# An expert's way back to the tokens: its products placed nine pieces after its last one instead of five

## The chip, the cores and the metric

The kernel runs on one core of one Trainium2 chip. The time is that of the device for one execution, in microseconds (us); three runs of the kernel before gave 1337.02, 1337.85 and 1338.05 us.

## What is computed

A trunk of two residual layers over 256 tokens of width 1024, in float32. Layer 0 is attention beside a short convolution and then a dense SwiGLU; layer 1 is a gated recurrence and then a mixture of experts: each token goes to two of eight SwiGLU experts. The change lies in the mixture of experts, of which the reference says

```
def moe_swiglu(h, w_router, w_gate, w_up, w_down):
    ...
    def expert_block(args):
        tok, e = args
        xb = xf[tok]
        hb = jax.nn.silu(xb @ w_gate[e]) * (xb @ w_up[e])
        return hb @ w_down[e]
    yb = lax.map(expert_block, (row_tok.reshape(n_blocks, MOE_BLOCK), blk_expert))
    y = yb.reshape(n_rows, D).astype(jnp.float32) * row_gate[:, None]
    out = jnp.zeros((T, D), jnp.float32).at[row_tok].add(y)
```

The last line is the one that matters here: an expert's rows, scaled by their gates, are added at their tokens.

## The kernel before

**Pieces and blocks.** The experts' stage begins about 500 us into the execution and takes the rest of it. An expert's hidden width of 3584 is cut into seven parts of 512, and a block is one part of one expert, 56 blocks in all. The loop at the end of `experts` walks a list of pieces; a block has twelve: g0 to g3 (gate), u0 to u3 (up) and d0 to d3 (the down products of the block ahead of it). A piece is half of a 1 MB load of weights. Three of the eight experts are heavy (up to 128 rows, three matmuls for each slice of weights: lines L240 to L242) and five light (up to 64 rows, whose high and low halves share one matmul, L1101 and L1102). After a lead of three heavy blocks the order is light, heavy, light, and again light, heavy, light, so two light blocks stand between heavy ones.

**Weights.** Weights are split into a high and a low part so that the fast float32 form of the matmul keeps its precision: ScalarE (ACT) writes the high part H (L260), VectorE (DVE) subtracts it from the weights and writes the low part L (L261). There are four pairs of H and L. `prepare` is called in the loop so that a load is split about four loads (eight pieces) ahead of its matmuls; ACT has to wait until TensorE (PE) has done with the pair that it is to overwrite. SyncE (SP) issues the loads; a tile of weights is free for the next load once DVE has subtracted.

**The order.** Every engine takes its instructions in the order in which the loop writes them. For a piece n the loop writes the matmuls of the piece, then what `follow` hangs on it, then what was put off to this n by `at(n, ...)`, then the `prepare` that is due. So DVE's work for a step that hangs on piece n stands in DVE's queue behind the subtraction of a load that PE will use about three to four loads later.

**Steps that share the two tiles z.** PSUM has two tiles with the tag z (`pz`), taken in turn. They are used by
- the turn of a finished hidden part, five pieces after u3, which is g0 of the next block: for a heavy block `turn`, four transposes (L1129), then a split of the result by ACT and DVE (L260 and L261 on a tile of 512 columns); for a light block `turn_light`, sixteen matmuls with an identity (L1140), then ACT's Silu (L1145) and DVE's product (L1146);
- the gathering of an expert's rows, and `factors` and `back` (L1082, L1091), a block ahead of an expert's start;
- `combine`, the step that the change moves: it takes a quarter of an expert's output, brings its rows back to the tokens with four matmuls of 256 columns (two each of L1170 and L1171) into a tile z, and DVE adds the tile to `x_sb` (L1173), which frees it.

**When an expert ends.** Its last down pieces d0 to d3 lie in the block that follows its last one. After d1 and after d3 `out_parts` scales half of the output (ACT L1162, DVE L1163). The four calls of `combine` are put off from there:

```
                end = n + BACK + 7 >= len(pieces)
                for j in R2:
                    at(n + (1 + j if end else BACK + 2 * j + i - 1), combine, p, i - 1 + j)
```

Counted from d1 with BACK at 5 they hang on the pieces 5, 7, 9 and 11 further on: g2, u0, u2 and d0 of the block after. Experts 1 and 0 end in blocks that follow each other, and so do 4 and 3: there eight calls stand in two light blocks. Experts 2 and 5 end alone, and their calls stand in a heavy block. Experts 7 and 6 are the last, and `end` gives them short distances.

Of the kernel before, what the change touches and what calls it, by code (L numbers as in the profile page):

```python
# [54 lines left out]
FIRST = 1  # L55
SECOND = 2
TURN = 5
BACK = 5

TURNS8 = N_RING + 2  # L60
TURNS4 = TURNS8 + 2
# [54 lines left out]
def body(ctx, tc, x_d, w_d, prm_d, bv_d, rt_d, out_d):  # L116
# [811 lines left out]
    def experts(rest):  # L928
# [249 lines left out]
        def at(n, fn, *a):  # L1178
            later.setdefault(min(n, len(pieces) - 1), []).append((fn, a))

        def follow(n):
# [22 lines left out]
            elif m == "d" and i % 2 and f == NF - 1:  # L1204
                out_parts(p, i // 2)
# [5 lines that stand above are left out]
# [152 lines left out]
```

## Time and profile before

| | |
|---|---|
| median of three runs | 1337.85 us |
| profiled execution: its own time | 1336.78 us |
| profiled execution: span of the trace | 1334.8 us |
| PE, DVE, ACT: busy share of the span | 97%, 85%, 73% |
| adds of `combine` (L1173) | 32, from 686.9 us to 1328.2 us |
| granted clock of TensorE, mean over the span | 0.994 of full speed |

The busy share of PE is not its share of useful work, since matmuls overlap in the trace: a wait is read from the bracket behind an instruction, which gives the idle time ahead of it and the instruction that ended it. Where an engine is busy without a break for tens of us it sets the pace there, or another engine hands it its work just in time.

### The profile page before, as it was taken

The numbers are of one execution on the slowest core, as the hardware profiler recorded it, in microseconds if no ns is written. First come the engines' busy times: TensorE is split into PE (matmuls) and PEld (weight loads), VectorE is DVE, ScalarE is ACT, GpSimd is POOL, SyncE is SP. The second block draws the span as 40 slices with busy tenths as digits, with TensorE's granted clock in tenths as the row PEclk, the third lists the DMA queues.
The fourth block names the chain that finished last, engine by engine and source line by source line (L and its number), as shares of the span: only waits on it lengthen the run. The fifth ranks groups of instructions, "written<-read, shape, count | busy, mean of one in ns | idle before, by whom it ended". The sixth has DMA issues, their size and how long they took to land.

```text
span 1334.8 us, 19883 instructions
## 1 busy us (share of the span) xinstructions
PE 1293.1 (97%) x7727; PEld 1134.4 (85%) x7727; DVE 1135.0 (85%) x1051; ACT 971.6 (73%) x937; POOL 4.2 (0%) x29
## 2 busy tenths in 40 slices
PE   8899999999998999999999999999999999999997
PEld 7799999999998877888877888878887888888885
DVE  6677655555688787999999999999989999999996
ACT  6455433444578687888888898889888898889883
POOL 1000000000000000000000000000000000000000
PEclk9899999999999999999999999999999999999999
DMA  7434545555443778999999999999999999999993
GB/s 302 174 127 158 190 177 176 186 190 189 138 179 107 273 273 325 400 421 422 421 416 381 416 421 420 415 406 422 420 422 393 390 422 421 422 406 423 421 420 121
DMA packets 61446, 427.19 MB, mean 320 GB/s; under 512 B 7200, under 2 KB 7200, under 8 KB 11296
## 3 DMA queue, kind: packets, MB, share of 16 engines
q1 hardware_dynamic: 60624, 425.22, 79.9%
q8 instruction: 62, 1.02, 0.3%
q10 hardware_dynamic: 720, 0.62, 0.1%
q14 instruction: 40, 0.33, 0.1%
HBM read 424.77 MB, written 1.05 MB: 319 GB/s over the span
## 4 chain that ended last, share of the span: by engine, by line
PE 76%; DVE 13%; issue 5%; ACT 4%; DMA 1%; SPq 0%; DVEq 0%; ACTq 0%
PE pw L240 11%; PE pw L241 11%; PE pw L242 10%; DVE L L261 9%; PE pw L1101 5%; PE pw L1102 5%; PE pz L1140 4%; PE pa L1101 3%; PE pa L241 3%; PE pa L1102 3%; PE pa L242 3%; PE pa L240 3%; PE pa L323 3%; PE pa L322 3%; PE pa L321 3%
## 5 line engine op out<-in xcount | busy, mean ns | idle before, releaser
L261 DVE TENSOR_TENSOR L<-w,H 128x2048 fp32r<-128x2048 f32 (+1 forms) x243 | 536.6, 2239 | 27.2 <-ACT H L260 27.0
L260 ACT ACTIVATE H<-w 128x2048 fp32r<-128x2048 f32 (+1 forms) x243 | 451.0, 1878 | 50.3 <-PE pw L242 19.0
L233 ACT ACTIVATE H<-w 128x1024 fp32r<-128x1024 f32 (+1 forms) x138 | 140.8, 1041 | 153.6 <-issue 140.6
L261 DVE TENSOR_TENSOR L<-b,H 128x2048 fp32r<-128x2048 f32 (+1 forms) x102 | 222.3, 2200 | 7.7 <-ACT H L260 7.7
L1101 PE MATMUL pw<-H,b 128*128 128x512 f32 x560 | 222.3, 397 | 0.0
L1102 PE MATMUL pw<-L,b 128*128 128x512 f32 x560 | 219.0, 391 | 0.2
L234 DVE TENSOR_TENSOR L<-w,H 128x1024 fp32r<-128x1024 f32 (+1 forms) x138 | 164.1, 1205 | 62.0 <-ACT H L233 62.0
L260 ACT ACTIVATE H<-b 128x2048 fp32r<-128x2048 f32 (+1 forms) x102 | 186.7, 1845 | 20.4 <-PE pw L242 9.6
L240 PE MATMUL pw<-b,H 128*128 128x256 f32 x672 | 191.7, 286 | 2.3 <-DVE b L600 1.1
L241 PE MATMUL pw<-b,H 128*128 128x256 f32 x672 | 191.4, 285 | 0.0
L242 PE MATMUL pw<-b,L 128*128 128x256 f32 x672 | 191.1, 284 | 0.0
L240 PE MATMUL pw<-H,b 128*128 128x512 f32 x336 | 135.0, 402 | 1.4 <-ACT b L1057 1.1
L241 PE MATMUL pw<-L,b 128*128 128x512 f32 x336 | 133.2, 397 | 1.2 <-DVE L L261 1.2
L240 PEld LDWEIGHTS pw<-b,H 128*128 128x128 f32 x672 | 129.7, 193 | 3.9 <-issue 3.1
L242 PE MATMUL pw<-H,b 128*128 128x512 f32 x336 | 131.8, 392 | 0.1
L241 PEld LDWEIGHTS pw<-b,H 128*128 128x128 f32 x672 | 129.7, 193 | 0.2
L242 PEld LDWEIGHTS pw<-b,L 128*128 128x128 f32 x672 | 129.8, 193 | 0.0
L1102 PEld LDWEIGHTS pw<-L,b 128*128 128x128 f32 x560 | 105.3, 188 | 21.8 <-DVE L L261 1.6
L1101 PEld LDWEIGHTS pw<-H,b 128*128 128x128 f32 x560 | 105.3, 188 | 20.2
L1101 PE MATMUL pa<-H,b 128*128 128x512 f32 x280 | 109.7, 392 | 0.0
L1102 PE MATMUL pa<-L,b 128*128 128x512 f32 x280 | 109.1, 390 | 0.0
L322 PE MATMUL pa<-b,H 128*128 128x256 f32 x352 | 99.4, 284 | 1.5 <-DVE b L261 1.5
(250 smaller groups left out, 1925.3 us busy)
## 6 DMA issues: line engine op xcount, KB each, us to landing
w<-in_w_dram SPq DMA_DIRECT2D x297, 1024.0 KB, 8.9
b<-in_w_dram SPq DMA_DIRECT2D x94, 1024.0 KB, 9.4
w<-in_w_dram SPq DMA_DIRECT2D x12, 512.0 KB, 11.2
b<-in_w_dram SPq DMA_DIRECT2D x8, 512.0 KB, 9.6
w<-in_w_dram SPq DMA_DIRECT2D x4, 768.0 KB, 8.0
x_sb<-in_x_dram SPq DMA_DIRECT2D x4, 256.0 KB, 7.7
out_dram<-x_sb SPq DMA_DIRECT2D x2, 256.0 KB, 3.1
out_dram<-x_sb ACTq DMA_DIRECT2D x2, 256.0 KB, 3.1
```

Of the source, the lines that this page charges most:

```text
L233: A.activation(h, w[:, c], AF.Copy)
L234: V.tensor_sub(l, w[:, c], h.bitcast(F32))
L240: T.matmul(o, a[0], b[0], start=first, stop=False)
L241: T.matmul(o, a[0], b[1], start=False, stop=False)
L242: ended[:] = [T.matmul(o, a[1], b[0], start=False, stop=last)]
L260: A.activation(oh, src, AF.Copy)
L261: V.tensor_sub(ol, src, oh.bitcast(F32))
L321: T.matmul(o, h[:, c], m[0][:, ks[i], :], start=f and d % 2 == 0, stop=False, skip_group_check=True)
L322: T.matmul(o, h[:, c], m[1][:, ks[i], :], start=False, stop=False, skip_group_check=True)
L1101: T.matmul(o, a, h, start=first, stop=False)
L1102: T.matmul(o, a, l, start=False, stop=last)
L1140: T.matmul(o[:, c:c + 64], src[:, k * P:(k + 1) * P], ii, start=True, stop=True)
```

## The change

One number that sets the order of the work:

```diff
--- before.py
+++ after.py
@@ -55,7 +55,7 @@
 FIRST = 1
 SECOND = 2
 TURN = 5
-BACK = 5
+BACK = 9
```

The four calls of `combine` now hang on the pieces 9, 11, 13 and 15 after d1: u2, d0 and d2 of the block after, and g0 of the one after that. The calls of experts 7 and 6 keep their places, since `end` holds for them with either number. So 24 of the 32 calls move, each with its four matmuls on PE and its add on DVE. No instruction is added or taken away, and no load changes its place among the loads.

On DVE, where experts 1 and 0 end: the stretch from behind the subtraction for d0 and d1 of a block to the product that belongs to the turn in g0 of the next block (L1146). `L` are the low parts of loads, `x_sb` is the sum that `combine` adds to. Before:

```order
L1173 TENSOR_TENSOR x_sb<-pz_6802,x_sb 128x512
L261 TENSOR_TENSOR L_6817<-w_6814,H_6816 128x2048
L1173 TENSOR_TENSOR x_sb<-pz_6825,x_sb 128x512
L261 TENSOR_TENSOR L_6838<-w_6835,H_6837 128x2048
L1173 TENSOR_TENSOR x_sb<-pz_6845,x_sb 128x512
L261 TENSOR_TENSOR L_6860<-w_6857,H_6859 128x2048
L1173 TENSOR_TENSOR x_sb<-pz_6869,x_sb 128x512
L1163 SCALAR_TENSOR_TENSOR b_895_6882<-pa_5250,gs_5084,b_894_6881 128x512
L261 TENSOR_TENSOR L_6888<-w_6885,H_6887 128x2048
L1163 SCALAR_TENSOR_TENSOR b_895_6882<-pa_5251,gs_5084,b_894_6881 128x512
L261 TENSOR_TENSOR L_6908<-b_899_6905,H_6907 128x2048
L1146 TENSOR_TENSOR b_904_6925<-pz_6916,b_904_6925 128x256
```

and now, at the same place:

```order
L261 TENSOR_TENSOR L_6811<-w_6808,H_6810 128x2048
L261 TENSOR_TENSOR L_6826<-w_6823,H_6825 128x2048
L1173 TENSOR_TENSOR x_sb<-pz_6833,x_sb 128x512
L261 TENSOR_TENSOR L_6848<-w_6845,H_6847 128x2048
L1173 TENSOR_TENSOR x_sb<-pz_6857,x_sb 128x512
L1163 SCALAR_TENSOR_TENSOR b_893_6870<-pa_5250,gs_5084,b_892_6869 128x512
L261 TENSOR_TENSOR L_6876<-w_6873,H_6875 128x2048
L1173 TENSOR_TENSOR x_sb<-pz_6885,x_sb 128x512
L1163 SCALAR_TENSOR_TENSOR b_893_6870<-pa_5251,gs_5084,b_892_6869 128x512
L261 TENSOR_TENSOR L_6902<-b_898_6899,H_6901 128x2048
L1173 TENSOR_TENSOR x_sb<-pz_6910,x_sb 128x512
L1146 TENSOR_TENSOR b_904_6925<-pz_6916,b_904_6925 128x256
```

The instructions are the same; each of the four adds has moved two subtractions back, and the third and the fourth now stand around the last subtraction ahead of L1146.

On PE, the end of g0 of the block after that, where the turn of a light block stands. `pz` are the tiles z in the order in which they are taken. Before, the turn follows the piece, and the latest `combine` was four pieces earlier:

```order
L1102 MATMUL pw_6911<-L_6838,b_512_5129 128x512
L1140 MATMUL pz_6916<-ii,b_879_6812 128x64 [waits DVE_49]
L1140 MATMUL pz_6916<-ii,b_879_6812 128x64 x3
L1140 MATMUL pz_6916<-ii,b_889_6855 128x64 [waits Activation_49]
L1140 MATMUL pz_6916<-ii,b_889_6855 128x64 x3
```

and now:

```order
L1102 MATMUL pw_6905<-L_6826,b_512_5129 128x512
L1170 MATMUL pz_6910<-b_568_5410,b_863_6748 128x256 [waits DVE_49]
L1171 MATMUL pz_6910<-b_568_5410,b_864_6749 128x256
L1170 MATMUL pz_6910<-b_568_5410,b_863_6748 128x256
L1171 MATMUL pz_6910<-b_568_5410,b_864_6749 128x256
L1140 MATMUL pz_6916<-ii,b_878_6806 128x64 [waits DVE_49]
L1140 MATMUL pz_6916<-ii,b_878_6806 128x64 x3
```

The fourth `combine` (tile 6910) now stands directly ahead of the turn (tile 6916), and the tile z that the turn takes is the one that the third `combine` (tile 6885) has filled two pieces earlier.

Where an expert ends alone, the same happens to a heavy block's turn. PE before:

```order
L1102 MATMUL pw_8266<-L_8202,b_1075_7679 128x512
L1129 MATMUL pz_8271<-ident,b_1181_8169 128x128 [waits DVE_49]
L1129 MATMUL pz_8271<-ident,b_1181_8169 128x128 x3
L1101 MATMUL pw_8266<-H_8201,b_1075_7679 128x512
L1102 MATMUL pw_8266<-L_8202,b_1075_7679 128x512
```

and now:

```order
L1102 MATMUL pw_8260<-L_8190,b_1075_7679 128x512
L1170 MATMUL pz_8265<-b_575_5442,b_1166_8094 128x256 [waits DVE_49]
L1171 MATMUL pz_8265<-b_575_5442,b_1167_8095 128x256
L1170 MATMUL pz_8265<-b_575_5442,b_1166_8094 128x256
L1171 MATMUL pz_8265<-b_575_5442,b_1167_8095 128x256
L1129 MATMUL pz_8271<-ident,b_1180_8163 128x128 [waits DVE_49]
L1129 MATMUL pz_8271<-ident,b_1180_8163 128x128 x3
```

Here too the fourth `combine` (tile 8265) comes between g0's products and the turn (tile 8271).

## Rows read from the trace of the kernel before

**Rows 1.** Chain that ended last, in time: start us, us, engine, tile, line

```profile
661.78 1.73 PE pz L1140 x16
...
712.85 1.73 PE pz L1140 x16
...
755.98 1.73 PE pz L1140 x16
...
847.06 1.73 PE pz L1140 x16
...
893.02 1.73 PE pz L1140 x16
...
982.71 1.73 PE pz L1140 x16
...
1033.78 1.73 PE pz L1140 x16
```

**Rows 2.** Windows: us, busy of PE, PEld, DVE, ACT, POOL; PEclk, DMA, GB/s

```profile
680.00:690.00 10.00, 7.97 (x40) 6.18 (x39) 10.00 (x8) 7.89 (x8) 0.00 (x0) 1.00 1.01 421
...
700.00:710.00 10.00, 9.23 (x46) 6.96 (x45) 10.00 (x8) 8.24 (x8) 0.00 (x0) 1.00 0.98 381
```

**Rows 3.** Timeline of DVE, experts 1 and 0: start us, us, line [idle before]

```profile
684.68 2.28 DVE L261 TENSOR_TENSOR L<-w,H 128x2048 fp32r<-128x2048 f32 x1
686.88 0.68 DVE L1173 TENSOR_TENSOR x_sb<-pz,x_sb 128x512 f32<-128x512 f32 x1
...
695.88 0.74 DVE L1163 SCALAR_TENSOR_TENSOR b<-pa,gs,b 128x512 fp32r<-128x512 f32 x1
...
701.60 0.41 DVE L1146 TENSOR_TENSOR b<-pz,b 128x256 f32<-128x256 f32 x1
701.93 2.28 DVE L261 TENSOR_TENSOR L<-b,H 128x2048 fp32r<-128x2048 f32 x1
...
721.60 2.29 DVE L261 TENSOR_TENSOR L<-b,H 128x2048 fp32r<-128x2048 f32 x1 [0.78 <-ACT H L260]
```

**Rows 4.** Timeline of PE, the same stretch

```profile
684.82 0.39 PE L1170 MATMUL pz<-b,b 128*128 128x256 f32 x1 [1.82 <-DVE b L261]
...
696.01 1.89 PE L1140 MATMUL pz<-ii,b 128*128 128x64 f32 x16
...
712.69 1.89 PE L1140 MATMUL pz<-ii,b 128*128 128x64 f32 x16
```

**Rows 5.** Timeline of ACT: the split behind the first turn

```profile
698.69 1.92 ACT L260 ACTIVATE H<-b 128x2048 fp32r<-128x2048 f32 x1 [0.36 <-PE pw L1101]
```

**Rows 6.** Timeline of DVE, then of PE, where expert 2 ends

```profile
853.76 2.28 DVE L261 TENSOR_TENSOR L<-w,H 128x2048 fp32r<-128x2048 f32 x1
...
864.79 0.60 PE L1129 MATMUL pz<-ident,b 128*128 128x128 f32 x4
865.14 0.47 PE L1101 MATMUL pw<-H,b 128*128 128x512 f32 x1
...
872.15 0.39 PE L240 MATMUL pa<-H,b 128*128 128x512 f32 x1
873.23 0.50 PE L241 MATMUL pa<-L,b 128*128 128x512 f32 x1 [0.69 <-DVE L L261]
```

**Rows 7.** Timeline of PE: other waits, and matmuls behind one

```profile
40.81 0.27 PE L460 MATMUL pa<-dmb,slope 128*128 128x128 bf16 x1 [3.32 <-DVE b L423]
...
503.26 0.66 PE L1091 MATMUL pz<-ident,b 128*128 128x128 f32 x4 [1.94 <-DVE gs L1085]
...
503.99 0.60 PE L241 MATMUL pw<-L,b 128*128 128x512 f32 x1
...
507.37 0.43 PE L241 MATMUL pw<-L,b 128*128 128x512 f32 x1
```

**Rows 8.** Windows as in rows 2, behind two of PE's waits

```profile
40.00:45.00 5.00, 3.59 (x16) 3.00 (x17) 4.82 (x14) 1.01 (x3) 0.00 (x0) 0.50 0.98 385
...
504.00:506.00 2.00, 2.00 (x6) 1.60 (x5) 0.00 (x0) 2.00 (x3) 0.00 (x0) 0.50 0.90 266
```

## The prediction, made before the changed kernel ran

> **What bounds the kernel now.** I read first the chain of work that ended last, in order of time, for the length of the experts' stage between equal places: the turns of light blocks. A light, heavy and light block without an expert's end take 755.98 - 712.85 = 43.13 us. The three in which experts 1 and 0 end take 712.85 - 661.78 = 51.07 us, those with the end of 4 and 3 1033.78 - 982.71 = 51.07 us, and the three in which expert 2 ends alone 893.02 - 847.06 = 45.96 us [rows 1]. So the steps at an expert's end cost some 8 us twice and 2.8 us twice (expert 5 repeats expert 2), and the change moves a part of them.
>
> Then the windows over the first of these places [rows 2]: DVE is busy all of the time, PE waits for 2.03 and 0.77 us out of 10, and the loads run at 381 GB/s in the second window against 421 in the first. There the weights wait for the engines, not the engines for the weights. Last the timelines. PE's largest wait is 1.82 us at 684.82, a product of `combine` that wants the tile z of the heavy block's turn, which DVE frees late [rows 4]. DVE runs without a break and is idle again for 0.78 us at 721.60, where it waits for ACT, and ACT for a pair that PE has yet to give back [rows 3]. So DVE paces the stretch from about 676 to 721 us, and PE what follows. Each of them can hold up the other: DVE holds PE by a tile z that isn't freed, and PE holds DVE by a pair that isn't given back.
>
> **The change part by part.** Nothing is added, so the 24 moved products cost nothing by themselves: 96 matmuls and 24 adds stand at other places. Their buffers (an expert's scaled output and its one-hot rows) are held four pieces longer, some 4 us; nothing asks for them until the next gathering, about 100 us on, so that is nothing too. Loads keep their order, and no queue but PE's, DVE's and ACT's own shifts. What the change makes is one wait and what it takes away is another.
>
> It takes away the wait of 1.82 us [rows 4] and some shorter ones, 2.8 us together [rows 2], since u2 and not g2 is the first place: the turn's tile has long been freed when the second product wants it.
>
> What it adds is at g0 of the block after. Tiles z are two and are taken in turn, so the turn in g0 takes the tile of the third product. Its add stands in DVE's queue behind the subtractions of loads for pieces that PE reaches only later; until now four to six pieces lay between, now two. I work out when DVE gets there from the durations in the trace, start to start: a subtraction 2.20 us (684.68 to 686.88), and 0.08 less than its own length for the others: an add 0.60, a scaling (L1163) 0.66, L1146 0.33 [rows 3].
>
> Experts 1 and 0, first turn. From 684.68 the new order has five subtractions, two adds and one scaling ahead of the third add: 5 x 2.20 + 2 x 0.60 + 0.66 = 12.86, so it starts at 697.54 and ends at 698.22. DVE isn't idle on the way: it wasn't before, and PE, with its wait of 1.82 gone, gives its pairs back earlier. PE is ready for the turn at about 695.3 (0.7 earlier than the 696.01 of before [rows 4], since of the 2.0 us of waits that go about 1.3 come back as waits for a subtraction or an add). So it waits about 3.0 us, and the turn starts at 698.28, which is 2.27 later than before.
>
> Second turn. PE gives back the pair of g0 and g1 after the turn (1.73 [rows 1]) and g1 (ACT's split came at 698.69, which is 0.95 after the turn's matmuls ended by that length [rows 5]); ACT then takes 1.92. Before, this H was there at 700.61, 1.3 us ahead of DVE's start at 701.93 [rows 3]. It is now there at 698.28 + 1.73 + 0.95 + 1.92 = 702.88: DVE is idle for 0.95. By the same reckoning it is idle for another 0.30 at the next split. From 702.88 to the third add of the second expert: five subtractions, two adds, a small split of 0.33 and that idle 0.30: 2.20 + 0.33 + 0.30 + 2.20 + 2.20 + 0.60 + 2.20 + 0.60 + 2.20 = 12.83, so it starts at 715.71 and ends at 716.39. PE needs 712.69 - 696.01 less the waits of 0.77, that is 15.9 us, from one turn to the next [rows 2, 4] and is ready at about 714.2, so it waits 2.2 to 2.3 us; the turn starts at 716.44 against 712.69 before [rows 4], **3.75 us later**. If DVE were idle nowhere it would be 2.45 us, which I take as the lower end. From there on PE sets the pace until the next expert's end (the 0.78 us in [rows 3] are DVE's wait for it), so all of it stays. It comes twice: 7.5 us, at the least 4.9.
>
> An expert that ends alone. From 853.76 [rows 6] the third add has ahead of it five subtractions, two adds, a product (0.60) and a small split: 5 x 2.20 + 1.20 + 0.60 + 0.33 = 13.13; it ends at 867.57. PE is ready at about 865.3 (half a us after the 864.79 of before, since the fourth product waits for the second one's add), waits 2.3 us and turns at 867.63. But this was not the last wait there: before, PE stood again at 873.23, for 0.69 us, for a subtraction [rows 6]. That one ends at the same time as before, since DVE's sum is the same. From 865.14 to 872.15 PE needs 7.0 us, of which about 0.5 are short waits for DVE that go. It is there at 867.63 + 0.35 + 6.5 = 874.5 against 872.15 + 0.69 + 0.2 = 873.0 of before: **1.5 us later**, twice: 3.0 us.
>
> Together 10.5 us (7.9 with the lower end).
>
> **TensorE's clock.** The six new waits last 3.0 us (two) and 2.3 us (four), from matmul to matmul; by the trace's way of counting, which starts at the modelled end of the matmul before, about 2.8 and 2.15. Behind a wait of 3.32 us, and behind one of 1.94, the granted clock is seen at half, 1.2 GHz [rows 7, 8]; behind the 1.82 it stays at 2.4 GHz [rows 2]. So the new waits are longer than one behind which it fell, but one instance of each is little to go by. Behind 503.26 the matmuls are long from 503.99 to 507.37 [rows 7]: 3.4 us at half the clock, which at the full one would have been at least 1.7; I take 1.5 as the cost. PE sets the pace behind each of these waits, so a fall is paid in full. I count three of six: 4.5 us; the bounds are none and six, 0 and 9 us.
>
> **The sum.** The profiled execution took 1336.78 us, of which its span is 1334.8. 1336.78 + 10.5 + 4.5 = 1351.8; the median of the three runs lies 1.07 above the profiled one, so 1352.9. Without idle time on DVE, which the first turn argues against but does not exclude, it would be some 2.6 less; I put the forecast between, at 1352.
>
> **The rivals.**
>
> *DVE is the bound and nothing else counts: no change.* DVE has the same instructions in the stretch, and it is busy in all of both windows [rows 2]. If only its sum mattered, waits of PE would be free and the time would stay at 1337.9. It decides if the H that follows a late turn still comes before DVE wants it, that is, if the turn is late by less than the 1.3 us that were to spare. The sum above says 2.27. That is why I think it fails, and this rests on PE's late return of pairs, of which the idle 0.78 us [rows 3] and ACT's 0.36 [rows 5] are the only signs in these rows.
> The Trainium skill has a rule that gives this rival's answer: its page Perfetto Trace Analysis, under Identifying the Most-Contended Engine, says to take the engine with the highest occupancy as the one that limits. In the window from 680 to 690 that is DVE with 10.00 of 10 [rows 2], and by that rule the time would be 1337.9 too.
>
> *The old waits go and no new one comes: faster.* PE's 1.82 us and the short waits make 2.0 + 0.8 = 2.8 us at an end of two experts [rows 2], twice 5.6: 1337.85 - 5.6 = 1332. It decides if the third add is done when PE arrives at the turn, which takes a DVE about 3 us further ahead than 684.68 shows. For it: PE waits for the turn's tile in a row of the trace, and the change clears exactly that. Against it: DVE has no idle time to get ahead, and the order shows the third add behind a further subtraction.
>
> *Slower, but by less.* If the length of the turns' delay is paid only in part (DVE's idle time absorbed in the 0.78 us that it has in every third block, or loads, at 421 GB/s in the first window [rows 2], being late elsewhere and catching up meanwhile), 4 to 7 us remain: 1342 to 1345.
>
> **How the numbers follow.** The forecast with its bounds (no fall of the clock and no idle DVE: 1337.85 + 7.9 = 1345.8; all six falls and all idle time: 1337.85 + 10.5 + 9 = 1357.4) has 0.74; slower by less 0.08; no change 0.10; faster 0.08. A measurement of this kernel tells about 0.2% from no change, 2.7 us. So slower has 0.82, the same 0.10, faster 0.08. The range from 1341 to 1359 leaves out the last two rivals, 0.18.
>
> **What would show it.** Right: PE's rows at g0 of the block after an expert's end have a wait for `x_sb` (L1173) of 2 to 3 us ahead of L1140 (four times) and L1129 (twice); the wait of 1.82 us is gone; DVE is idle for about 1 us behind the first turn and about 2 behind the second; the steps of [rows 1] are 51.07 + 3.75 and 45.96 + 1.5 us, or 1.5 us more for each fall, and steps without an end still take 43.1. Windows with a granted clock under 1.00 behind the turns count the falls. Wrong: turns that start on time, steps of [rows 1] that have not grown, or DVE without idle time behind a late turn.

## The result, and the profile of the changed kernel

| | before | after |
|---|---|---|
| median, us | 1337.95 (1337.02 to 1342.43, 4 runs) | 1355.82 (1355.04 to 1357.34, 4 runs) |
| profiled execution: time, span, mean granted clock | 1336.78, 1334.8, 0.994 | 1357.34, 1355.4, 0.984 |

The changed kernel is slower: ratio 1.0128, 95% interval 1.0107 to 1.0149; the medians are 17.9 us apart. In a second set of runs the medians were 1339.57 (16 runs) and 1358.19 (5 runs), ratio 1.0127 (1.0095 to 1.0159). The runs of one kernel lie in two groups (in the second set eight of the kernel before took 1335.6 to 1337.9 us and eight 1341.3 to 1343.2), so a median of few runs can be off by some us, while the steps between equal places in the trace, used below, hold nothing of what came before them.

Where the time is, the chain that ended last shows, in time order: start us, length us, engine, tile, line. These are the light blocks' turns, as in [rows 1].

```profile
661.34 1.73 PE pz L1140 x16
697.84 3.68 PE pz L1140 x16
719.47 2.00 PE pz L1140 x16
751.09 1.73 PE pz L1140 x16
...
842.17 1.73 PE pz L1140 x16
892.33 1.73 PE pz L1140 x16
905.70 1.73 PE pz L1140 x16
...
995.39 1.73 PE pz L1140 x16
1031.90 3.29 PE pz L1140 x16
1053.53 2.00 PE pz L1140 x16
1083.55 1.73 PE pz L1140 x16
...
1173.43 1.73 PE pz L1140 x16
1220.77 1.73 PE pz L1140 x16
```

Experts 1 and 0: from 661.34 to 719.47 it is 36.50 + 21.63 = 58.13 us, where [rows 1] have 51.07. With 4 and 3 it is 36.51 + 21.63 = 58.14. The step behind the second turn is 31.62 in the first case and 30.02 in the second. It was 29.76 in the kernel before: that is the 43.13 of [rows 1] less a light step of 13.37, as 892.33 to 905.70 still is. Expert 2: 842.17 to 892.33 is 50.16, and expert 5's 1173.43 to 1220.77 is 47.34; both were 45.96 (these steps begin one turn earlier than the one in [rows 1], and hold the same work). So the six ends took 7.06 + 1.86, 7.07 + 0.26, 4.20 and 1.38 us more: 21.8 together. The experts' stage began 0.4 us earlier in this execution, and the spans differ by 20.6. In the last 80 us of the kernel before ACT waits five times for a load, 2.7 us together, and in those of the changed kernel never; I take the 0.8 us that are left for that.

What PE waited for in the experts' stage, then the turns in the timeline of PE (the bracket is the idle time ahead, and what ended it):

```profile
PE pz L1140 <- DVE x_sb L1173: 9.6, 4, 2.7
...
PE pz L1129 <- DVE x_sb L1173: 4.1, 2, 2.1
```

```profile
697.84 3.68 PE L1140 MATMUL pz<-ii,b 128*128 128x64 f32 x16 [2.72 <-DVE x_sb L1173]
...
703.13 0.63 PE L1101 MATMUL pw<-H,b 128*128 128x512 f32 x1
...
719.47 2.00 PE L1140 MATMUL pz<-ii,b 128*128 128x64 f32 x16 [2.06 <-DVE x_sb L1173]
...
876.11 1.12 PE L1129 MATMUL pz<-ident,b 128*128 128x128 f32 x4 [2.06 <-DVE x_sb L1173]
```

The columns of the first view are the total in us, how many, and the longest. There are six waits of 2.72 (twice) and 2.06 us (four times), all for an add of `combine`, all ahead of a turn. The wait of 1.82 us for L261 [rows 4] is gone. The timeline of DVE at the end of experts 1 and 0, with one row of ACT, answers to [rows 3, 5]:

```profile
697.11 0.68 DVE L1173 TENSOR_TENSOR x_sb<-pz,x_sb 128x512 f32<-128x512 f32 x1
...
704.88 2.29 DVE L261 TENSOR_TENSOR L<-b,H 128x2048 fp32r<-128x2048 f32 x1 [2.49 <-ACT H L260]
...
725.78 2.29 DVE L261 TENSOR_TENSOR L<-b,H 128x2048 fp32r<-128x2048 f32 x1 [3.23 <-ACT H L260]
...
702.94 1.91 ACT L260 ACTIVATE H<-b 128x2048 fp32r<-128x2048 f32 x1 [1.00 <-PE pw L1101]
```

The third add ends at 697.79 and the turn starts 0.05 us behind it. DVE then stands idle for 2.49 us at a place where it went on without a break before (701.93 in [rows 3]), since ACT had to wait for PE and wrote H at 702.94 and not at 698.69. The windows of the same stretch (busy time of PE, PEld, DVE, ACT and POOL, then granted clock, DMA share and GB/s), to be read beside [rows 2]:

```profile
690.00:700.00 10.00, 6.92 (x34) 5.66 (x33) 10.00 (x9) 4.89 (x4) 0.00 (x0) 0.89 1.01 419
700.00:710.00 10.00, 10.00 (x41) 8.47 (x41) 5.57 (x6) 6.40 (x6) 0.00 (x0) 0.77 0.68 257
...
698.00:700.00 2.00, 2.00 (x10) 2.00 (x11) 2.00 (x2) 0.00 (x0) 0.00 (x0) 0.50 1.02 406
...
704.00:706.00 2.00, 2.00 (x9) 1.65 (x8) 1.12 (x1) 0.96 (x2) 0.00 (x0) 0.83 0.62 258
```

From 700 to 710 DVE is busy for 5.57 us of 10 (10.00 before), and the loads run at 257 GB/s (381 before). TensorE is at 1.2 GHz from about 698 to 704.7, and a matmul of 512 columns takes 0.63 us (703.13), where [rows 6] have 0.39 to 0.50.

### The profile page after: what moved, and what is told of

Its sections match the earlier page's. It is cut to its first block, busy times and chain, and to the rows that moved or that the text cites. A ratio compares the mean times of both kernels' runs of the same rounds, so it can differ in the third digit from the quotient of the medians.

```text
span 1355.4 us, 19881 instructions
## 1 busy us (share of the span) xinstructions
PE 1303.4 (96%) x7727; PEld 1143.5 (84%) x7727; DVE 1136.4 (84%) x1051; ACT 970.0 (72%) x937; POOL 4.2 (0%) x29
## 4 chain that ended last, share of the span: by engine, by line
PE 72%; DVE 16%; issue 6%; ACT 4%; DMA 0%; SPq 0%; DVEq 0%; ACTq 0%
DVE L L261 11%; PE pw L240 10%; PE pw L241 10%; PE pw L242 10%; PE pw L1101 6%; PE pw L1102 5%; PE pz L1140 4%; PE pa L241 3%; PE pa L242 3%; PE pa L240 3%; PE pa L1101 3%; PE pa L1102 3%; PE pa L323 3%; PE pa L322 3%; PE pa L321 3%
## 5 line engine op out<-in xcount | busy, mean ns | idle before, releaser
L261 DVE TENSOR_TENSOR L<-w,H 128x2048 fp32r<-128x2048 f32 (+1 forms) x243 | 537.0, 2242 | 34.5 <-ACT H L260 34.4
L261 DVE TENSOR_TENSOR L<-b,H 128x2048 fp32r<-128x2048 f32 (+1 forms) x102 | 222.4, 2203 | 19.1 <-ACT H L260 19.1
L1101 PE MATMUL pw<-H,b 128*128 128x512 f32 x560 | 225.9, 403 | 0.0
L1102 PE MATMUL pw<-L,b 128*128 128x512 f32 x560 | 222.0, 396 | 1.2 <-DVE L L261 1.2
L240 PE MATMUL pw<-H,b 128*128 128x512 f32 x336 | 135.6, 404 | 1.3 <-ACT b L1057 1.1
L241 PE MATMUL pw<-L,b 128*128 128x512 f32 x336 | 133.8, 398 | 1.2 <-DVE L L261 1.2
L242 PE MATMUL pw<-H,b 128*128 128x512 f32 x336 | 132.6, 395 | 0.1
```

The lines of the kernel that those rows point to most:

```text
L240: T.matmul(o, a[0], b[0], start=first, stop=False)
L241: T.matmul(o, a[0], b[1], start=False, stop=False)
L242: ended[:] = [T.matmul(o, a[1], b[0], start=False, stop=last)]
L261: V.tensor_sub(ol, src, oh.bitcast(F32))
L1101: T.matmul(o, a, h, start=first, stop=False)
L1102: T.matmul(o, a, l, start=False, stop=last)
```

## Experiments

Steps below are those between the turns' starts in the chain. "Pair" is the sum of the two steps of an end of two experts (51.07 before), "single" the step of an expert that ends alone (45.96 before). The runs of the kernel before that each set shares had medians of 1337.14 (19 runs: e1 to e4), 1337.24 (29 runs: e5 to e8) and 1339.57 (16 runs: e9 and e10).

### The change in parts: only the pairs, only the single ends

e1 puts experts 0, 1, 3 and 4 nine pieces on and leaves 2 and 5 at five (the first of the added lines); e2 does the opposite (the second).

```diff
-                    at(n + (1 + j if end else BACK + 2 * j + i - 1), combine, p, i - 1 + j)
+                    at(n + (1 + j if end else (9 if p in (0, 1, 3, 4) else 5) + 2 * j + i - 1), combine, p, i - 1 + j)
...
+                    at(n + (1 + j if end else (9 if p in (2, 5) else 5) + 2 * j + i - 1), combine, p, i - 1 + j)
```

> Only the products of experts 0, 1, 3 and 4, which end in pairs, stand nine pieces on; those of 2 and 5 stay at five. My theory (a wait of the turn for the third product's add, paid in full, and falls of the clock behind it) gives each pair 3.75 us and each fall about 1.5 to 3: the trios with a pair's end 51.1 + 3.75 plus their falls, those with expert 2 or 5 unchanged at 46.0, the time 1350 to 1354. A rival by which the delay comes from every moved product alike (24 of them for 17.6 us) gives 16 / 24 of it: 1349.6 and 46.0 us for the single ends too; the trios tell the two apart, not the sum.

> Only the products of experts 2 and 5, which end alone, stand nine pieces on. My theory: 1.5 us for each and 1.5 to 3 us for a fall of the clock behind their turn if there is one: 1341 to 1345, trios 46.0 + 1.4 without a fall, about 49 with one. The rival of equal shares gives 8 / 24 of 17.6 us: 1343.7.

Measured: e1 1353.30 us (1353.05 to 1353.62, 4 runs), ratio 1.0117 (1.0089 to 1.0146); pairs 36.50 + 21.62 and 36.49 + 21.57, single ends 45.95 as before. e2 1343.58 us (1339.28 to 1348.63, 10 runs), ratio 1.0032 (1.0012 to 1.0051); single ends 47.31 and 47.32, pairs 51.10 and 51.08. Each group of products delays its own turns and no others; some 16 us belong to the pairs. In the profiled execution of e2 no fall of the clock followed the single ends' turns, so 1.35 and 1.36 us are what the wait alone costs there. (The median of e2 is more than 2 x 1.36 above the kernel before; its runs spread over 9 us, and its profiled execution had lost 5 us before the experts' stage began. How much of the rest are falls at the single ends can't be read from times alone.)

### The fourth product alone, and the fourth product moved away from the turn

The order of the change shows the fourth product directly ahead of the turn. e3 puts only that one late (places 5, 7, 9, 15); e4 takes only that one out of the way (9, 11, 13, 14, so it stands behind d3 and a piece lies between it and the turn).

```diff
-                    at(n + (1 + j if end else BACK + 2 * j + i - 1), combine, p, i - 1 + j)
+                    at(n + (1 + j if end else (5, 7, 9, 15)[i - 1 + j] + 1 - i), combine, p, i - 1 + j)
...
+                    at(n + (1 + j if end else (9, 11, 13, 14)[i - 1 + j] + 1 - i), combine, p, i - 1 + j)
```

> The first three products stand at 5, 7 and 9 as before, the fourth alone at 15 (g0 of the next block, directly ahead of the turn). My theory: the turn takes the tile of the third product, which is now six pieces old, so there is no wait for its add; 1338, within 2 us. The rival by which it is the crowding at g0 (two steps on the tiles z in a row) that delays the turn expects the turn late by 2 us or more at all six ends, and 1343 or more.

> The first three products at 9, 11 and 13 as in the changed kernel, the fourth at 14 (d3), so nothing but the turn stands at g0. My theory: the turn still takes the tile of the third product, two pieces old, and waits 2 to 3 us for its add: 1350 to 1357. The rival by which crowding at g0 makes the delay expects 1338 to 1341.

Measured: e3 1340.03 us (1337.88 to 1345.25, 10 runs), ratio 1.0023 (1.0005 to 1.0042), pairs 51.82 and 51.78, single ends 45.93. e4 1354.18 us (1347.93 to 1357.24, 4 runs), ratio 1.0132 (1.0097 to 1.0167), single ends 47.32. The timeline of PE in e3, at the first turn:

```profile
701.52 1.90 PE L1140 MATMUL pz<-ii,b 128*128 128x64 f32 x16
706.34 0.35 PE L1170 MATMUL pz<-b,b 128*128 128x256 f32 x1 [1.03 <-DVE x_sb L1173]
```

With the fourth product alone ahead of it the turn starts without a wait. The fourth add delays only the next expert's product, by 1.03 us here and by 2.08 in the second pair, and the pairs grow by 0.7. The time, 1340.03, is just outside the 1338 within 2 us that were expected, and below the rival's 1343. The chain of e4 at the first pair, and its waits:

```profile
661.36 1.73 PE pz L1140 x16
697.86 2.00 PE pz L1140 x16
716.28 2.00 PE pz L1140 x16
746.28 1.73 PE pz L1140 x16
```

```profile
PE pz L1170 <- DVE x_sb L1173: 8.3, 10, 1.3
PE pz L1140 <- DVE x_sb L1173: 4.9, 4, 1.8
```

The fourth product now waits itself, and the turn waits less but comes no earlier (36.50 again): it still wants the tile of the third. The first pair of e4 had no fall of the clock, and so shows what the waits cost without one: 36.50 + 18.42 = 54.92, and 30.00 for the step behind; (54.92 - 51.07) + (30.00 - 29.76) = 4.09 us.

### The third product in another tile

This run decides whether the tile is the cause or the place. All products stay nine pieces on, and their adds stand in DVE's queue where the change put them; but the third goes into one of the accumulators of the gate and up products (tag w), so the turn takes the tile z of the second product, whose add has been queued two pieces earlier.

```diff
-            o = zz()
+            o = pw() if i == 2 and p < 6 and not rest else zz()
```

> The changed kernel, every instruction at its changed place, but the third product goes into a tile of the tag w (the gate and up sums take these in turn, and none is open at d2) instead of a tile z. The turn then takes the tile of the second product, which is four pieces old. My theory: the wait of the turn for the third add is gone, and with it the delay and the falls: 1337 to 1341. The rival by which it is the later place of 24 products and adds that costs the time expects the 1355.8 of the changed kernel.

Measured: 1336.51 us (1335.75 to 1341.81, 12 runs), ratio 0.9995 (0.998 to 1.001). Pairs 33.12 + 17.51 = 50.63 with 30.01 behind, single ends 45.95. The turn in the timeline of PE and the third add in that of DVE:

```profile
695.65 2.00 PE L1140 MATMUL pz<-ii,b 128*128 128x64 f32 x16
...
713.24 2.00 PE L1140 MATMUL pz<-ii,b 128*128 128x64 f32 x16 [1.03 <-DVE x_sb L1173]
```

```profile
698.37 0.68 DVE L1173 TENSOR_TENSOR x_sb<-pw,x_sb 128x512 f32<-128x512 f32 x1
```

The first turn starts at 695.65 without a wait, 3.4 us before the third add is over. The second waits 1.03 us, now for the add of the second product, whose tile it takes. The whole loss of the change is gone with one tile; the time is 0.5 us below the 1337 to 1341 that were expected.

### The waits filled with matmuls

Here the four matmuls of each moved fourth product, the one directly ahead of the turn, are run six times over into the same tile. The result is the same, DVE gets the same work, and the turn still can't start before the third add is over, but PE works for most of the time in which it stood still.

```diff
-            for j in range(2):
+            for j in range(2) if i < 3 or p > 5 else [0, 1] * 6:
```

> The changed kernel with the matmuls of the fourth product done six times over instead of once, into the same tile with the same result, so that PE works through its wait for the tile of the third product: 2.3 us of matmuls more ahead of the turn. My theory: the turns start when the third add ends, as in the changed kernel, so these matmuls cost nothing, and the clock does not fall behind the turns: the six ends cost 2 x 3.9 + 2 x 1.4 us against before and the time is 1347 to 1350. The rival by which the whole of the 17.6 us is the wait for DVE and the clock counts for nothing expects 1355 or more, and for the matmuls added up to 6 x 2.3 us on top.

Measured: 1348.01 us (1347.71 to 1352.51, 4 runs), ratio 1.0076 (1.0057 to 1.0094). Pairs 36.49 + 18.78 and 36.49 + 18.75, with 29.74 behind; single ends 47.42 and 47.43. PE, DVE, and windows of e5:

```profile
703.13 2.00 PE L1140 MATMUL pz<-ii,b 128*128 128x64 f32 x16 [0.32 <-DVE x_sb L1173]
```

```profile
707.88 2.29 DVE L261 TENSOR_TENSOR L<-b,H 128x2048 fp32r<-128x2048 f32 x1 [1.01 <-ACT H L260]
710.83 4.49 DVE L261 TENSOR_TENSOR L<-w,H 128x2048 fp32r<-128x2048 f32 x2 [0.32 <-ACT H L260]
...
727.07 2.29 DVE L261 TENSOR_TENSOR L<-b,H 128x2048 fp32r<-128x2048 f32 x1 [2.42 <-ACT H L260]
```

```profile
700.00:710.00 10.00, 9.68 (x62) 8.61 (x61) 8.99 (x8) 5.86 (x6) 0.00 (x0) 1.00 1.01 412
```

The first turns come as late as in the changed kernel (36.49 against 36.50), and no window of the experts' stage between 530 and 1340 us is below 2.4 GHz. So the two parts of the loss come apart: the delay is 1348.01 - 1337.24 = 10.8 us, the clock 1355.82 - 1348.01 = 7.8 us (by the two ratios, 1.0128 - 1.0076, it is 7.0). The sum of the steps without a fall, from e4 and e2, says the same of the first part: 2 x 4.09 + 2 x 1.36 = 10.9. The steps of e5 itself make 2 x 4.18 + 2 x 1.47 = 11.3, since its added matmuls end 0.2 us after the add at the second turn and delay it a little themselves.

### Seven pieces

```diff
-BACK = 5
+BACK = 7
```

> The number at 7: products at u0, u2, d0 and d2. The third add then stands behind four subtractions, not five, and ends at about 695.4 to 696.1 on the clock of the trace before, where the turn stood at 696.01; PE's old wait at u0 is gone too. My theory: no wait of more than 0.5 us ahead of the turns and no gain either, since DVE sets the pace in the stretch: 1337 to 1340. A rival by which the delay grows with each piece that the products are moved expects half of it, 1346.

Measured: 1337.70 us (1337.04 to 1341.75, 12 runs), ratio 1.0001 (0.999 to 1.0013); pairs 51.46 and 51.48, single ends 45.94 and 45.98. The longest wait for an add is one of a product, not of a turn:

```profile
PE pz L1170 <- DVE x_sb L1173: 5.7, 6, 1.4
```

Between seven and nine the loss sets in: at seven the turn takes the tile of the third product too, but with two pieces more between them.

### What paces the pairs in the kernel before: fewer adds

If DVE's sum is the pace there, as the prediction read from [rows 2, 3], fewer adds must shorten the pair. With five pieces as before, one product brings back both experts of a pair (matmuls of both accumulate in one tile, one add instead of two: eight adds fewer in the kernel).

```diff
+            if p in (1, 4) and not rest:
+                return
+            ps = {0: (1, 0), 3: (4, 3)}.get(p, (p,)) if not rest else (p,)
...
-                T.matmul(o[:, j * S:(j + 1) * S], yh[:, d], pts[p], start=True, stop=False)
-                T.matmul(o[:, j * S:(j + 1) * S], yl[:, d], pts[p], start=False, stop=True)
+                for q in ps:
+                    yh, yl = yp[q]
+                    T.matmul(o[:, j * S:(j + 1) * S], yh[:, d], pts[q], start=q == ps[0], stop=False)
+                    T.matmul(o[:, j * S:(j + 1) * S], yl[:, d], pts[q], start=False, stop=q == ps[-1])
```

> The number at 5. The products of expert 1 are done together with those of expert 0, and those of 4 with 3: for each quarter both experts' matmuls go into one tile z, and one add takes the sum to the tokens, so that 8 of the 32 adds fall away. My theory that DVE sets the pace where two experts end: 4 adds of 0.60 us less at each pair, 51.1 becomes 48.7, and the time 1332.5 to 1334. If instead the waits for the tiles z set the pace there, the eight matmuls at a place make PE's stay longer and the time does not change by more than 1 us.

e9 has these lines, the third product in the other tile, and nine pieces. (A pair is one light expert, 1 or 4, and one heavy, 0 or 3, not two light ones as the expectation says.)

> Nine pieces as in the changed kernel, with both remedies at once: the third product of an expert goes into a tile of the matmuls' own accumulators (as in the run of e8), and where two light experts end one behind the other, one product brings back both (as in e7, eight adds fewer). Theory (DVE paces the pair ends, and nine pieces cost time only through the turn's tile): the two savings add, since one takes adds from DVE and the other takes PE's wait away: pair 51.07 - 1.93 (e7) - 0.44 (e8) = 48.7 us, single ends 45.95 as in e8, so 4.7 us less than the kernel before in the experts' stage; about 1333 us, or as e7 where the clock falls in the early stage. Rival (what e8 saved is DVE's wait that e7 has removed already): pair 49.1, as e7, and the time that of e7, 1337.15 in the median. A second rival: with one product less to spread the adds over, products at nine pieces bring PE a new wait for a tile; the steps are longer than e7's.

Measured: e7 1337.15 us (1332.38 to 1339.22, 12 runs), ratio 0.9985 (0.997 to 0.9999); e9 1331.81 us (1331.46 to 1337.22, 11 runs), ratio 0.9957 (0.9939 to 0.9975). The chain at the first pair, of e7 and then of e9:

```profile
666.89 1.73 PE pz L1140 x16
716.03 1.73 PE pz L1140 x16
```

```profile
664.12 1.74 PE pz L1140 x16
...
712.86 1.73 PE pz L1140 x16
```

The pair is 49.14 in e7, 1.93 less than 51.07; four adds of 0.60 each are 2.4. In e9 it is 48.74, as the two savings added give (51.07 - 1.93 - 0.44 = 48.70). e7 alone does not settle what paces the pair, since PE's waits for a tile z are gone in it too. But e8 loses the wait of 1.82 us with all its adds in place, and gains 0.44. The window over the first pair, of the kernel before and then of e9, says the same: PE stands still for 1.25 us in e9 and not for 2.80, and DVE is busy for all of the 40 us in both.

```profile
676.00:716.00 40.00, 37.20 (x192) 30.33 (x191) 40.00 (x31) 32.14 (x26) 0.00 (x0) 1.00 1.00 403
676.00:716.00 40.00, 38.75 (x202) 32.56 (x202) 40.00 (x27) 33.83 (x27) 0.00 (x0) 1.00 1.01 421
```

So DVE does pace the pairs, and e9 is faster than both kernels: 26 us below the changed one in the same set of runs (1358.19, e10), and 0.4% (0.25 to 0.6%) below the one before.

The time of e7 missed its forecast of 1332.5 to 1334 in the median. The profiled execution of e7 took 1337.72 us. Its first light turn in the chain is at 534.05, where that of the kernel before is at 528.95, so it had lost 5.1 us ahead of all the work that e7 alters. The steps show the gain, and this time hides it.

### The changed kernel again

> The changed kernel once more, to see which of its two results is usual: its profiled execution had four falls of the clock behind the six new waits and 10.9 us for them, while its median against that of the kernel with the waits filled makes 7.8 us. Theory (whether a given wait lets the clock fall differs from one execution to the next, and the waits themselves do not): the steps without falls are the same to 0.1 us (36.5 and 18.4 or 21.6 for a pair, 47.3 or 50.2 for a single end), the falls stand behind other ones of the six waits, and the time is 1350 to 1358 us. Rival (each place has its own fixed answer): falls behind the same four waits, with the same lengths, and the same steps to 0.1 us.

Measured: 1358.19 us (1355.27 to 1364.78, 5 runs). The median is just above the 1350 to 1358 that were expected. The waits are the same to the tenth (9.6 in four, 4.1 in two), the falls are not. The first single end, and the step behind the second turn of the first pair:

```profile
883.22 0.66 PE L1129 MATMUL pz<-ident,b 128*128 128x128 f32 x4 [2.06 <-DVE x_sb L1173]
```

```profile
882.00:884.00 2.00, 0.78 (x6) 0.75 (x7) 2.00 (x3) 0.09 (x1) 0.00 (x0) 1.00 1.03 401
```

```profile
725.04 3.68 PE pz L1140 x16
758.21 1.73 PE pz L1140 x16
```

The heavy turn at 883.22 waited 2.06 us, as the one at 876.11 in the first profile did, and ran its transposes in 0.66 us at the full clock, where the other took 1.12. The step from 725.04 to 758.21 is 33.17 us, where the first profile had 31.62 and the other pair 30.02. What each fall cost, in us, as the step less the same step without one (18.42 and 30.00 from e4, 47.33 from e2 and the changed kernel; with the 18.78 of e5 the falls behind first turns cost 0.4 less each):

| turn, and its wait | first profile | second profile |
|---|---|---|
| 1 and 0, first turn: 2.72 | 3.2 | 3.2 |
| 1 and 0, second: 2.06 | 1.6 | 3.2 |
| 2: 2.06 | 2.8 | none |
| 4 and 3, first: 2.72 | 3.2 | 2.9 |
| 4 and 3, second: 2.06 | none | 1.6 |
| 5: 2.06 | none | 1.6 |
| together | 10.8 | 12.5 |

The waits belong to the order of the work; whether a fall follows a wait of 2.06 us, and which length it has, differs between executions of one kernel.

## Why the prediction was right, and where it was off

**The cause was right.** The turn waits for the tile of the third product, whose add stands behind subtractions for pieces that come later. e8 shows it: same places, another tile, and the loss is gone. e3 and e4 exclude the fourth product, which stands next to the turn.

**First turn of a pair.** The prediction put it at 698.28; it came at 697.84 in an execution that was 0.44 us earlier in this stage (661.34 against 661.78 in [rows 1]). The wait was 2.72 (2.8 foreseen).

**Second turn.** DVE's idle time was put at 0.95 and 0.30 us behind the first turn, and about 2 behind the second. In e5, with no fall to lengthen it, it was 1.01, 0.32 and 2.42. A pair without falls costs 4.09 us; 3.75 were foreseen. The lower end, 2.45, rested on a DVE that is never idle (by the prediction's own terms it is 3.75 - 0.95 - 0.30 = 2.50), and for its sake the forecast of 1352 was put 0.9 us below the sum of 1352.9. That was a hedge on a step which the working had right.

**Single ends.** 1.35 to 1.47 us each (1.5 foreseen). The waits of the single ends' and of the second turns, four in all, were 2.06 us (2.15 foreseen).

**The sum of the delays** was put at 10.5 us; e5 against the kernel before has 10.8.

**The clock** is the term that was mis-sized: 4.5 us foreseen, 7 to 8 in the medians and 10.8 and 12.5 in the two profiled executions. The number of falls, three of six, was too low (four and five in the profiles), and above all the price of one, 1.5 us, was that of a short fall. It was worked out from the one stretch in [rows 7], 3.4 us of slow matmuls from 503.99 to 507.37. The other fall in the same rows was at half the clock for all of the 5 us from 40 to 45 [rows 8], so that row showed that a fall can be longer than 3.4 us (it lasted 6.8, by the granted clock in slices of 2 us from 38 to 48). All six falls behind a wait of 2.7 us in the profiles of the changed kernel and of e1 lasted about 6.8 us and cost 2.9 to 3.2. The bounds of 0 and 9 us held for the medians, not for the profiled executions.

**The rivals.** No change was to hold if the turn's delay stayed below the 1.3 us that H had to spare. The delay was 2.27 us (697.84 + 0.44 - 696.01), and DVE was idle for 4.43 us of the 10 from 700 to 710, the fall of the clock included. The rival was right in what paced the pair (e7: fewer adds, a shorter pair) and missed that a busy engine can be made to wait by the one that it feeds. The Trainium skill, in Perfetto Trace Analysis under Identifying the Most-Contended Engine, calls the engine with the highest occupancy the most contended one. Read as a rule for the time, as the prediction read it for this rival, that gave 1337.9 us; the measured time does not agree. Faster: PE's old wait of 1.82 us did go, and brought nothing. In e8, where it is gone too and only the second turn waits (1.03 us), the pair is 0.44 us shorter and the step behind it 0.25 longer, since DVE's sum sets the pace there: not the 2.8 us that this rival counted.

## What to carry to other kernels

Where two steps share a rotating buffer, a step that is moved later hands its late release to whoever takes that buffer next: count the instructions ahead of the release in the releasing engine's queue, and not the distance to the step itself. An engine at 100% in a window says that its own sum is the pace as long as its inputs come; a delay of its supplier beyond the lead that they have turns into idle time on it, and the lead can be read off one pair of rows (H at 700.61, wanted at 701.93). A gap on TensorE ahead of work that TensorE paces is to be priced with the fall of the clock behind it, by the longest fall in the trace and not by one instance; repeated matmuls that left the result as it was, put into the gap, took that price away here.

## What the runs showed of the hardware

**Falls behind short waits, not in every execution.** All six waits of 2.7 us in the profiles of the changed kernel (two) and of e1 were followed by a stretch at 1.2 GHz; of the waits of 2.06 to 2.08 us in these profiles and in e2 and e3, six of thirteen; of those of 1.92 to 1.99 us ahead of L1091 between 502 and 511, one in each of the twelve profiles, six; and of those of 1.78 to 1.87 us in the kernel before and in e2, e3 and e4, three of nine. One of these three is the wait of [rows 4], in e2: the same 1.82 us ahead of the same instruction, and the clock fell, where in the kernel before it stayed at 1.00 [rows 2]:

```profile
690.14 0.39 PE L1170 MATMUL pz<-b,b 128*128 128x256 f32 x1 [1.82 <-DVE b L261]
```

```profile
692.00:694.00 2.00, 2.00 (x6) 1.57 (x5) 2.00 (x3) 1.85 (x1) 0.00 (x0) 0.50 1.01 422
```

The Trainium skill, in TensorE: Matmul & The Clock Gate, What's actually happening, says that the number of slow matmuls at the start of one kernel varies from run to run. In the middle of this kernel the two profiles of the changed kernel show the like, with four falls and five.

**Two lengths.** The falls behind these waits lasted some 3.4 us or some 6.8, by the granted clock in slices of 2 us, and cost about 1.6 or 3 us where PE set the pace. (At the turn at 876.11 of the first profile the slices from 874 to 884 have 0.83, 0.50, 0.50, 0.50 and 0.96. A slice that is at half the clock throughout has 0.50, so these five hold 6.8 us of it.) In e2 the fall at 692 cost nothing, since DVE paces the pair: it took 51.10 us, and the other pair of e2, without a fall, 51.08.

**Falls ahead of the change's stage.** The same happens in the first 530 us of all these kernels, which the change doesn't touch. The first light turn of the chain is at 528.47 in the first profile of the changed kernel and at 534.14 in the second. The second is at half the clock from 452 to 458, and the first is not. The twelve profiles divide in this way: the six with a fall between 450 and 459 reach that turn at 531.3 to 534.2 us, the six without one at 528.5 to 529.8. So some 5 us of a time can come from a stage that two kernels share. For the runs that weren't profiled this is not shown, since these have only their mean clock.
